# Twelve-head input loads issued as two DMAs of half a row each, in a q·kᵀ kernel

## The chip, the cores and the metric

The kernel runs on one core of a Trainium2 chip. The metric is device time in microseconds (us) of the whole program; less is better. The core has a matrix engine (PE), a vector engine (DVE), a scalar engine (ACT), a general engine (POOL) and a synchronising engine (SP), each with its own stream of instructions; semaphores order them. Data moves between the large memory (DRAM) and the core's on-chip memory (128 partitions) through 16 DMA engines. A DMA is issued by an instruction on an engine's queue: here SP's, which appears in the profile as q1, or ACT's, which appears as q10.

## The reference

For 8 x 12 = 96 heads, each with a q and a k of 1024 rows by 64 columns in float32, the product of all rows with all rows:

```python
def reference(q, k):                      # (8, 12, 1024, 64) each
    return np.einsum('bhid,bhjd->bhij', q, k).astype(np.float32)
```

The inputs are 50.33 MB and the output, 96 matrices of 1024 x 1024 float32, is 402.65 MB.

## The kernel before

The 96 heads are cut into blocks of 2, 2, 4, 8, 8 and then six times 12 heads (`sizes`). For each block, q and k are loaded as float32, cast to float16 by POOL, transposed so that the 64 columns lie on partitions, and multiplied head by head by PE; ACT copies the products from PE's accumulators to an output buffer, and SP issues one store of 4 MB for each head. The kernel writes its own semaphore counts: `Engine.run` makes an instruction wait for a list of events, `Landing` counts the 16 increments that each DMA gives to its semaphore, and `Ring` hands out buffers in turn together with the events that must be over before a buffer is written again.

What matters for the change and for the steps of the prediction:

- **Loads.** `Block.load` (lines 152 to 163) takes an input buffer from the ring `inputs`, which has two (`x_sb`, 24 KB in each partition), waits until its last reader is done, and issues one DMA that puts `R` consecutive rows into each partition (line 160). For twelve heads this is 12 x 1024 / 128 = 96 rows of 64 float32, 24,576 consecutive bytes in each partition. The event that stands for the load is the buffer's semaphore with its count so far. For the first three blocks the data goes into an output buffer that isn't in use yet (lines 330 to 343); those loads, and the two of the first block of eight, are issued by SP at the start. All others are issued by ACT through `next_load` (line 350), q first and then k.
- **When a load is issued.** `LOADS` (line 81) and line 410 put it behind the second group of products of a head: heads 4 and 6 of a block of eight, heads 6 and 8 of a block of twelve. It fetches what the block after the next will use.
- **Casts.** `cast_quads` (line 201) has POOL write float16 into one of two buffers `half`, once the load has landed (line 215) and the transpose that read this buffer before is done. A block of twelve has four chunks, two of q and two of k, each of four casts.
- **Transposes.** `transpose_quads` (line 222) has DVE transpose a chunk (line 230). It also waits for the last matmul of the block two before, since both use the same buffers `qT` and `kT`. They are written into the program during the heads of the block before (line 409).
- **Products.** `scores` (line 239) issues for each head four groups of two row tiles: a weight load (line 309) and two matmuls of 512 columns (line 312) for each tile, then one copy of 128 x 2048 by ACT (line 289). The first group of a block waits for that block's transposes. The copies wait until the output buffer is free, that is until the store of three heads earlier has landed; there are three output buffers. SP waits for the copies and issues the store (line 302).

Of the kernel before, what the change touches and what calls it, by code (L numbers as in the profile page):

```python
# [8 lines left out]
P = 128  # L9
# [50 lines left out]
def kernel(  # L60
# [8 lines left out]
    B, H, S, D = q.shape  # L69
# [4 lines left out]
    flat = [x.rearrange("b h s d -> (b h s) d") for x in (q, k)]  # L74
# [61 lines left out]
    class Block:  # L136
# [15 lines left out]
        def load(self, x, eng, landing=None):  # L152
            events = []
            if self.raw[x] is None:
                buf, events, self.raw_busy[x] = inputs.next()
                self.raw[x] = buf[:, : self.elems]
                landing = input_landing[id(buf)]
            src = flat[x][self.first * S : (self.first + self.N) * S]
            eng.wait(events)
            dma = eng.eng.dma_start(  # L160
                out=self.raw[x], in_=src.rearrange("(p r) d -> p (r d)", p=P)
            )
            self.landed[x].append(landing.start(dma))

        def load_head(self, n, x, eng, landing):
            start = (self.first + n) * S
# [189 lines left out]
    for x in range(2):  # L356
# [7 lines left out]
                out=ident,  # L364
                in_=ident,
# [98 lines left out]
```

## Time and profile before

| | |
|---|---|
| median of 3 runs | 1062.36 us (1062.35 to 1063.84) |
| the profiled execution | 1062.55 us, of which the span from the first to the last instruction is 1060.4 us |
| PE busy | 700.5 us (66% of the span), 1568 instructions |
| ACT busy | 697.0 us (66%) |
| DVE busy | 470.6 us (44%) |
| POOL busy | 345.3 us (33%) |
| DMA traffic | 453.19 MB in 17,583 packets, mean 427 GB/s over the span |
| one copy of 128 x 2048 on ACT (line 289) | 1.86 us, 384 copies (four smaller ones on DVE) |
| store of one head, issue to landing | 21.7 us (median of 96) |
| load of twelve heads, issue to landing | 22.0 us for q, 21.9 us for k (medians of 6 each) |

The page divides the span into 40 slices and gives each engine's busy share in tenths; the row DMA is the mean share of the 16 DMA engines. A packet is what one DMA engine moves in one piece. For the large transfers here, that is one partition's share of a DMA: 32,768 bytes for a store of one head, 24,576 bytes for a load of twelve heads. Each DMA ends with one packet of 4 bytes on each of the 16 engines, the increments of its semaphore. In the list of groups, and in the timeline, a line names the engine, the line of the program, the operation and the buffers, then the number of instructions; in square brackets stands how long the engine was idle ahead of it, and what ended that.

### The profile page before, as it was taken

The page shows a single profiled execution, that of the slowest core. Times are in us where ns is not written, and L with a number is a line of the kernel's source. Part 1 is how long each engine was busy: PE and PEld are TensorE (multiplying, and loading weights), DVE is VectorE, ACT ScalarE, POOL GpSimd, SP SyncE. Part 2 cuts the span into 40 slices and gives each one's busy share as a digit, 9 for nine tenths or more (in the row PEclk, how much of TensorE's full clock was granted, in tenths as well). Part 3 has the DMA queues.
Part 4 walks back from the last instruction along what each step waited for, and adds up shares of the span by engine and source line. Part 5 has one row for each costly group of instructions (what it writes and reads, how often), then busy time and mean ns, then how long its engine had stood idle before and what let it go on. Part 6 is the DMA issues. An engine that isn't in the chain of part 4 may idle for free.

```text
span 1060.4 us, 3258 instructions
## 1 busy us (share of the span) xinstructions
PE 700.5 (66%) x1568; PEld 127.3 (12%) x800; DVE 470.6 (44%) x43; ACT 697.0 (66%) x386; POOL 345.3 (33%) x158
## 2 busy tenths in 40 slices
PE   6876755765577557774577855777557777778770
PEld 2111100110111001110011100111001111111110
DVE  2998602991795006960069600795007950000000
ACT  4766755755678557775577755776557777777771
POOL 7667216436360430704307053160531600000000
DMA  9999999999999999999999999999999999999997
GB/s 376 434 435 434 432 419 430 435 428 431 433 432 428 428 435 430 430 431 423 438 431 429 433 431 434 434 429 422 426 432 435 429 434 434 434 435 430 431 434 336
DMA packets 17583, 453.19 MB, mean 427 GB/s; under 512 B 1952, under 2 KB 1952, under 8 KB 2976
## 3 DMA queue, kind: packets, MB, share of 16 engines
q1 hardware_dynamic: 14976, 410.00, 90.0%
q10 hardware_dynamic: 2592, 42.99, 9.7%
q8 instruction: 9, 0.15, 0.0%
q14 instruction: 6, 0.05, 0.0%
HBM read 50.33 MB, written 402.65 MB: 427 GB/s over the span
## 4 chain that ended last, share of the span: by engine, by line
DMA 71%; ACT 17%; PE 7%; DVE 2%; issue 1%; POOL 0%; ACTq 0%; SPq 0%
DMA out_dram<-o_sb 70%; ACT o_sb L289 17%; PE ps_all L312 7%; DVE kT L230 1%; DVE qT L230 1%; DMA o_sb<-in_q_dram 0%; PE ps_all L244 0%; POOL qT L180 0%; DVE kT L251 0%; ACT kT L251 0%; ACTq L36 0%; SPq L168 0%; SPq L459 0%; SPq L97 0%
## 5 line engine op out<-in xcount | busy, mean ns | idle before, releaser
L289 ACT COPY o_sb<-ps_all 128x2048 f32<-128x2048 f32 (+1 forms) x384 | 694.7, 1859 | 333.0 <-DMA out_dram<-o_sb 301.6
L312 PE MATMUL ps_all<-kT,qT 64*128 64x512 f16 x1536 | 696.4, 617 | 327.8 <-ACT o_sb L289 322.4
L211 POOL CAST half<-x_sb 32x3072 f16<-32x3072 f32 (+1 forms) x128 | 323.4, 2527 | 491.6 <-DMA x_sb<-in_q_dram 242.2
L230 DVE STREAM_TRANSPOSE qT<-half 128x3072 f16<-128x3072 f16 (+1 forms) x16 | 222.9, 14132 | 370.0 <-PE ps_all L312 370.0
L309 PEld LDWEIGHTS <-qT 64*128 64x128 f16 x768 | 124.2, 162 | 896.8 <-issue 889.2
L230 DVE STREAM_TRANSPOSE kT<-half 128x3072 f16<-128x3072 f16 (+1 forms) x16 | 224.2, 14217 | 2.8 <-POOL half L211 2.8
L230 DVE STREAM_TRANSPOSE kT<-kT 128x1024 f16<-128x1024 f16 x2 | 9.3, 4836 | 0.0
L230 DVE STREAM_TRANSPOSE qT<-qT 128x1024 f16<-128x1024 f16 x2 | 9.2, 4784 | 0.0
L211 POOL CAST qT<-o_sb 32x1024 f16<-32x1024 f32 x8 | 8.3, 1034 | 1.2 <-DMA o_sb<-in_q_dram 0.8
L211 POOL CAST kT<-o_sb 32x1024 f16<-32x1024 f32 x8 | 8.3, 1033 | 0.5
L251 DVE COPY qT<-ps_all 128x1024 f16<-128x1024 f16 x2 | 2.5, 1225 | 11.0 <-PE ps_all L244 11.0
L289 DVE COPY o_sb<-ps_all 128x1024 f32<-128x1024 f32 x4 | 4.9, 1225 | 4.4 <-PE ps_all L312 4.4
L244 PE MATMUL ps_all<-ident,qT 128*128 128x128 f16 x16 | 2.1, 310 | 6.7 <-POOL qT L180 6.6
L251 ACT COPY kT<-ps_all 128x1024 f16<-128x1024 f16 x1 | 1.0, 1012 | 4.7 <-PE ps_all L244 4.7
L180 POOL CAST qT<-o_sb 128x512 f16<-128x512 f32 x4 | 2.3, 612 | 3.6 <-DMA o_sb<-in_q_dram 3.6
L251 DVE COPY kT<-ps_all 128x1024 f16<-128x1024 f16 x1 | 1.2, 1225 | 4.4 <-PE ps_all L244 4.4
L251 ACT ACT_TABLE_LOAD x1 | 1.3, 1283 | 2.8 <-issue 2.8
L244 PE MATMUL ps_all<-ident,kT 128*128 128x128 f16 x16 | 2.0, 305 | 0.7 <-ACT o_sb L289 0.7
L180 POOL CAST kT<-o_sb 128x512 f16<-128x512 f32 x4 | 2.3, 613 | 0.4 <-DMA o_sb<-in_q_dram 0.4
L244 PEld LDWEIGHTS ps_all<-ident,qT 128*128 128x128 f16 x16 | 1.5, 140 | 6.9 <-POOL qT L180 6.9
L244 PEld LDWEIGHTS ps_all<-ident,kT 128*128 128x128 f16 x16 | 1.5, 136 | 3.3 <-POOL qT L211 1.6
L359 POOL MEMSET ident<- 128x128 f16 x1 | 0.2, 205 | 0.5 <-SPq L97 0.5
(5 smaller groups left out, 0.7 us busy)
## 6 DMA issues: line engine op xcount, KB each, us to landing
out_dram<-o_sb SPq DMA_DIRECT2D x96, 4096.0 KB, 21.7
x_sb<-in_q_dram ACTq DMA_DIRECT2D x6, 3072.0 KB, 22.0
x_sb<-in_k_dram ACTq DMA_DIRECT2D x6, 3072.0 KB, 21.9
x_sb<-in_q_dram SPq DMA_DIRECT2D x1, 2048.0 KB, 14.6
x_sb<-in_k_dram SPq DMA_DIRECT2D x1, 2048.0 KB, 19.6
x_sb<-in_q_dram ACTq DMA_DIRECT2D x1, 2048.0 KB, 18.3
x_sb<-in_k_dram ACTq DMA_DIRECT2D x1, 2048.0 KB, 19.1
o_sb<-in_k_dram ACTq DMA_DIRECT2D x4, 256.0 KB, 4.7
```

The source lines that it names most:

```text
L180: lambda: nc.gpsimd.tensor_copy(out=rows[:, :, h], in_=self.raw[x][:, h * n : (h + 1) * n].rearrange("p (r d) -> p r d", d=D),),
L211: lambda: nc.gpsimd.tensor_copy(out=dst[q0 : q0 + 32].rearrange("p (r d) -> p r d", d=32), in_=raw[32 * b : 32 * b + 32, c * m : (c + 1) * ...
L230: lambda: nc.vector.transpose(out=dst, in_=buf.rearrange("p (r i) -> p r i", i=32)),
L244: lambda: nc.tensor.transpose(t_ps[:, t], rows[:, t], ident),
L251: lambda: copy(out=dst, in_=t_ps.rearrange("c t m -> c m t")), [done]
L289: lambda: (nc.vector.tensor_copy if by_dve else nc.scalar.copy)(out=dst, in_=ps[:, : w * S]),
L309: return nc.tensor.ldweights(stationary, tile_position=(at, 0))
L312: return nc.tensor.add_instruction(mybir.InstMatmult(name=nc.get_next_instruction_name(), ins=[nc.tensor.lower_ap(moving), nc.tensor.lower ...
L359: cleared = gps.run(lambda: nc.gpsimd.memset(ident, 0.0))
```

## The change

Only `Block.load` is changed. Where a block has more than eight heads, the load is issued as two DMAs in direct succession on the same queue: the first brings the first half of each partition's row of 24,576 bytes, the second the rest. Both count on the same semaphore, and the event that readers wait for is the count after the second. Loads of smaller blocks are issued as before.

```diff
-            src = flat[x][self.first * S : (self.first + self.N) * S]
+            src = flat[x][self.first * S : (self.first + self.N) * S].rearrange(
+                "(p r) d -> p (r d)", p=P
+            )
             eng.wait(events)
-            dma = eng.eng.dma_start(
-                out=self.raw[x], in_=src.rearrange("(p r) d -> p (r d)", p=P)
-            )
-            self.landed[x].append(landing.start(dma))
+            pieces = 2 if self.N > 8 else 1
+            m = self.elems // pieces
+            for i in range(pieces):
+                dma = eng.eng.dma_start(
+                    out=self.raw[x][:, i * m : (i + 1) * m], in_=src[:, i * m : (i + 1) * m]
+                )
+                landed = landing.start(dma)
+            self.landed[x].append(landed)
```

## The prediction, made before the changed kernel ran

> **What bounds the kernel now.** I read the page's slices first, then its table of queues and its chain of waits, then the windows of the stages, then vector engine and loads in the timeline. The slices and queues, from the page:
>
> ```profile
> DMA  9999999999999999999999999999999999999997
> DMA packets 17583, 453.19 MB, mean 427 GB/s; under 512 B 1952, under 2 KB 1952, under 8 KB 2976
> q1 hardware_dynamic: 14976, 410.00, 90.0%
> q10 hardware_dynamic: 2592, 42.99, 9.7%
> DMA 71%; ACT 17%; PE 7%; DVE 2%; issue 1%; POOL 0%; ACTq 0%; SPq 0%
> out_dram<-o_sb SPq DMA_DIRECT2D x96, 4096.0 KB, 21.7
> x_sb<-in_q_dram ACTq DMA_DIRECT2D x6, 3072.0 KB, 22.0
> ```
>
> The 16 DMA engines are busy in every slice, and the two queues' packets fill 90.0 + 9.7 = 99.7% of the span. ACT's 17% and PE's 7% of the chain are no second bound: while ACT refills one output buffer, two stores stand on q1. The packet records say so more sharply: from about 4 us to 1053 us all 16 engines always have a packet in hand. They end one by one from 1053.3 to 1058.6 us, and the last store lands at 1059.1. So the time is the packet time of the engine that ends last, and an edit counts by the DMA engine time that it adds.
>
> The windows lie over the six pairs of loads (131-186 and so on) and the store-only stretches between:
>
> ```profile
> core 0: us, PE busy (x) PEld busy (x) DVE busy (x) ACT busy (x) POOL busy (x), PEclk, DMA share, GB/s
> 96.00:131.00 35.00, 25.74 (x58) 4.70 (x29) 25.18 (x3) 24.41 (x14) 15.10 (x8) 1.00 1.00 432
> 131.00:186.00 55.00, 29.45 (x65) 5.17 (x32) 6.38 (x1) 29.09 (x16) 21.92 (x8) 1.00 1.01 428
> ...
> 388.00:468.00 80.00, 57.78 (x128) 10.34 (x64) 61.29 (x4) 58.15 (x32) 21.92 (x8) 1.00 1.00 433
> 468.00:520.00 52.00, 29.30 (x65) 5.20 (x32) 0.44 (x1) 29.08 (x16) 21.92 (x8) 1.00 1.00 423
> ```
>
> Both kinds are full (share 1.00), yet a stage with loads moves less: weighted by length the six give 427.5 GB/s, the store-only windows 432.6. That is 1.2% of 316 us, or 3.7 us: the only slack in the DMA time that this change can touch.
>
> **The change, part by part.** Twelve loads (six q, six k, of blocks of twelve heads) become 24 DMAs; bytes, order and buffers stay, and the other engines' instructions stand as before.
>
> 1. Packets. A load of twelve heads is 128 packets of 24,576 bytes, eight on each engine. Median packet times in the records are 312 ns for 8,192 bytes, 611 for 16,384, 912 for 24,576 and 1213 for 32,768: 300 ns for every 8 KB, and 12 ns beside them. By that line 12,288 bytes take about 462 ns. The next packet starts 4 ns before the last one's record ends (stores start every 1209 ns), so a packet holds its engine for 458 ns: two are 916, one of 24 KB is 908. Each engine has 12 x 8 = 96 such pieces: 96 x 8 ns = 0.77 us.
>
> 2. Semaphore writes. Each DMA ends with one packet of 4 bytes on each engine. It is recorded with 9 ns, and the next store's data starts 6 ns after it started: 12 more cost about 0.08 us.
>
> 3. The second issue on ACT's queue.
>
> ```profile
> 159.86 1.86 ACT L289 COPY o_sb<-ps_all 128x2048 f32<-128x2048 f32 x1 [5.02 <-DMA out_dram<-o_sb]
> 159.91 0.33 ACTq L160 DMA_DIRECT2D x_sb<-in_k_dram  x1
> 161.62 1.87 ACT L289 COPY o_sb<-ps_all 128x2048 f32<-128x2048 f32 x1
> ```
>
> The issue (0.33 us) runs while the copy before it runs; a second still ends by 160.6, before the next copy at 161.62. Taken: nothing. Without that cover it were 12 x 0.334 = 4.0 us of ACT, which has 2.2 to 5 us idle for a store in each head. SP's queue, which issues the stores, gets no new instruction.
>
> 4. Later landings. In the records q1 and q10 alternate packet by packet on an engine: eight load packets with eight stores between them make 8 x (0.908 + 1.209) = 16.9 us, and the first load's packets run from 136.1 to 152.2. With 16 pieces it is 16 x (0.458 + 1.209) = 26.7 us, so q lands some 10 us later, and k, queued behind it, also about 10. Who waits is POOL's casts, and for them DVE:
>
> ```profile
> 153.79 22.34 POOL L211 CAST half<-x_sb 32x3072 f16<-32x3072 f32 x8 [40.59 <-DMA x_sb<-in_q_dram]
> 179.62 30.95 DVE L230 STREAM_TRANSPOSE qT<-half 128x3072 f16<-128x3072 f16 x2 [55.60 <-PE ps_all L312]
> 210.15 31.14 DVE L230 STREAM_TRANSPOSE kT<-half 128x3072 f16<-128x3072 f16 x2
> 272.06 30.95 DVE L230 STREAM_TRANSPOSE qT<-half 128x3072 f16<-128x3072 f16 x2 [30.77 <-PE ps_all L312]
> ```
>
> POOL's first chunk would be ready at about 175 instead of 165; DVE takes it at 179.6, since it waits for PE. Should DVE start late all the same, this block's transposes end at 241.3 and the block before leaves PE at 272: 30.8 us of cover, some 70 us in later blocks. Beyond it PE would stall for the excess, and the queues stay fed for the two stores already issued. Taken: nothing.
>
> 5. Collisions of loads and stores. In the records the 24 KB packets have a mean of 931 ns against 912; stores in the load stages 1232 against 1214 elsewhere. (1536 x 19 + 1711 x 18) / 16 engines = 3.8 us per engine, which agrees with the windows. No row shows it for 12 KB packets, so I bound it: at best it goes, -3.8 us; at worst it doubles with the packets, +3.8. The long packets stand in the first ten us of a load, more after a store-only stretch (0.25 to 0.76 us of engine time for q) than for the k behind it (0 to 0.16): they go with the start of reading, and the second piece brings no pause and so no new start. I take 0, the row as it is.
>
> Sum: 0.77 + 0.08 = +0.85 us of engine time, all of it on the bound. The profiled execution took 1062.55 us, its span 1060.4, so 2.15 lie around it, which don't change; it stands 0.2 above the median of 1062.36. Forecast: span 1061.2, median 1063.2.
>
> [...]
>
> **The rivals.**
>
> *Collisions go with the number of load packets (slower).* Place: the engines during the loads. Price: up to 3.8 us on top, 1063.2 + 3.8 = 1067.0. For it: each read among stores is a chance to be held up, there are twice as many, and reading lasts 27 us instead of 17. Against it: the second half of a load shows hardly any long packet. It decides from a growth of a third: 0.85 + 1.3 passes 0.2%.
>
> *Thinner reading collides less (faster).* The loads' share of engine time in such a stage falls from 0.908/2.117 = 43% to 0.458/1.667 = 27%. If collisions go with the density of reads, the 3.8 us may nearly go: 1063.2 - 3.8 = 1059.4. It must save over 3 us to pass 0.2%. What it could add is the skew: the 16 landings of a store lie 1.6 us apart before the first loads and 5.5 at the end, partly through the loads; the last engine ends some 3.5 us after the mean. Against it: even with no collision left the gain is 0.3%.
>
> *A fixed cost for each DMA stands open.* If the second DMA waited for the first to land, engines idle: from the last 24 KB packet's end to the landing it is 152.2 to 153.7, 1.5 us; twelve make 18 us, 1081. Against it: q1 has stores queued which would use that time, and the 6 ns above.
>
> *The change doesn't do what it says.* If the two pieces were made into the same 24 KB packets, the time stays at 1062.4. The packet's size now equals the row's run exactly, so I doubt it.
>
> **How the numbers follow.** 0.2% of the time is 2.1 us, about what a measurement of this kernel tells from no change: the bounds are 1060.2 and 1064.5. Chances: forecast 0.46, no change in packets 0.04, together 0.50 within; more collisions 0.28, fixed cost or a wait that I hold to be covered 0.05, together 0.33 slower; fewer collisions and less skew 0.17 faster. The predicted time is the forecast's, 1063.2, with 1061.5 to 1064.5 for this case alone. The range takes both ends of the collisions, 1059.4 to 1067.0, and leaves out the fixed cost.
>
> **What would show it.** q10 with 1536 + 192 = 1728 more packets and the same 42.99 MB; DMA share still 9 in every slice; packets of 12 KB near 462 ns (over 475 the first step is wrong); issue to landing near 32 us instead of 22 for the second pieces; DVE's waits still for PE and not for POOL; no idle of PE for DVE in the blocks of twelve. GB/s in the load windows judges the collisions: about 426 for the forecast, below 422 for more, near 430 for fewer. The prediction is wrong if the DMA row drops below 9 in a slice before the last, or if load windows of equal bytes change their length by over 3 us in sum.

## The result: 0.67% slower, and the profile after

| | before | changed |
|---|---|---|
| median of 6 runs | 1063.01 us | 1069.70 us (1068.22 to 1072.10) |
| ratio to before, 95% interval | | 1.0067 [1.0057, 1.0077] |
| profiled execution, its span | 1062.55, 1060.4 | 1070.06, 1067.9 |

The change costs 6.7 us. The page of the changed kernel, with the rows shown of before (queue rows: packets, MB, share of 16 engines; issue rows: count, KB each, median us to landing):

```profile
DMA  9999999999999999999999999999999999999997
DMA packets 19311, 453.19 MB, mean 424 GB/s; under 512 B 2144, under 2 KB 2144, under 8 KB 3168
q1 hardware_dynamic: 14976, 410.00, 89.9%
q10 hardware_dynamic: 4320, 42.99, 9.5%
DMA 71%; ACT 17%; PE 7%; DVE 2%; issue 1%; POOL 0%; ACTq 0%; SPq 0%
out_dram<-o_sb SPq DMA_DIRECT2D x96, 4096.0 KB, 22.1
x_sb<-in_q_dram ACTq DMA_DIRECT2D x12, 1536.0 KB, 25.4
```

q10 has 1728 packets more for the same bytes, so the loads are split as described. The DMA engines are as full as before, and the chain has the same shares: no new wait in it, the same transfers take longer. q1 didn't change at all in packets or bytes, yet its share of a span that is 7.5 us longer is nearly the same: 90.0% of 1060.4 us are 954 us, 89.9% of 1067.9 are 960. The stores' own packets have become longer, by some 6 us. That is the first reading to take from this pair of pages.

The windows of the changed kernel (same columns as before; the stages with loads are longer now):

```profile
96.00:131.00 35.00, 25.75 (x58) 4.68 (x29) 25.22 (x3) 24.52 (x14) 15.11 (x8) 1.00 1.00 429
131.00:194.00 63.00, 35.20 (x79) 6.16 (x39) 16.14 (x2) 36.38 (x20) 22.41 (x9) 1.00 1.01 427
...
404.00:474.00 70.00, 51.66 (x115) 9.20 (x57) 61.41 (x4) 50.91 (x28) 21.94 (x8) 1.00 1.00 432
474.00:538.00 64.00, 36.77 (x82) 6.50 (x40) 0.28 (x1) 36.39 (x20) 21.94 (x8) 1.00 1.00 420
```

Weighted over all six, the load stages last 380 us (316 before) at 423.6 GB/s (427.5), the store-only ones move 431.8 (432.6). Against the store-only rate the load stages lose 7.2 us where they lost 3.7.

The timeline shows that the later landings found their cover: first POOL and DVE around the first split load, then ACT at the issue of a k load.

```profile
163.89 22.36 POOL L217 CAST half<-x_sb 32x3072 f16<-32x3072 f32 x8 [50.66 <-DMA x_sb<-in_q_dram]
177.85 30.91 DVE L236 STREAM_TRANSPOSE qT<-half 128x3072 f16<-128x3072 f16 x2 [53.85 <-POOL half L217]
208.34 31.14 DVE L236 STREAM_TRANSPOSE kT<-half 128x3072 f16<-128x3072 f16 x2
272.74 30.90 DVE L236 STREAM_TRANSPOSE qT<-half 128x3072 f16<-128x3072 f16 x2 [33.25 <-PE ps_all L318]
```

```profile
157.87 1.87 ACT L295 COPY o_sb<-ps_all 128x2048 f32<-128x2048 f32 x1 [6.28 <-DMA out_dram<-o_sb]
157.92 2.15 ACTq L165 DMA_DIRECT2D x_sb<-in_k_dram  x2
159.63 1.88 ACT L295 COPY o_sb<-ps_all 128x2048 f32<-128x2048 f32 x1
161.68 1.87 ACT L295 COPY o_sb<-ps_all 128x2048 f32<-128x2048 f32 x1 [0.17 <-PE ps_all L318]
```

DVE's first transpose of that block is released by POOL now instead of by PE, but the block's transposes end at 239.5 and the block before leaves PE at 272.7. The two issues take 2.15 us on ACT's queue instead of twice 0.33; the next copies still start in step (159.63), and the third waits 0.17 us for PE, as before.

**Where the 7.5 us of the profiled pair are**, from the records of single packets. What a record lasts beyond the median of its size is called excess here, summed and divided by 16 engines.

```
us per engine                                   before   changed
excess in the load stages: stores of 32 KB        2.07      7.64
                           load packets           1.87      0.21
excess in all records of 8 KB and more            5.3      10.2
mean end of the 16 engines (last store)         1055.5    1060.9
end of the last engine                          1059.1    1066.6
```

A packet of 12,288 bytes takes 460 ns and the next starts 4 ns before its end, so the two cost 912 where one of 24 KB cost 908: 0.4 us for 96 pieces, with the semaphore writes 0.45. The collisions grew by about 4 us in the load stages and moved: they stood half on the load packets, now they stand on the stores. The mean engine ends 5.4 us later, and the last engine stands 5.7 us behind the mean instead of 3.6. Together 7.5.

Within the load stages the excess has a place. The packets of an engine can be told apart by joining each to the one that ends as it starts (where two engines' packets end within a few ns, this can exchange them). One engine of the changed kernel, start in us, length in ns, queue and bytes:

```
748.378  1744  q1  32768     eighth packet of a store
750.118   460  q10 12288
750.574     9  q1  4         that store's semaphore write
750.580   460  q10 12288
751.036  1213  q1  32768     next store
```

In load stages the eighth packets of a store are some 150 to 160 ns over 1213 on the mean, the seventh 30 to 37 and the first two no more than 3. Without load packets beside them eighth packets have next to no excess (under 5 ns on the mean). Around a store's end that lies between two load packets (the eighth packet, the load packets ahead of and behind the semaphore write) the excess is 220 ns on the mean of 185 such ends before and 218 ns of 352 after. The mean price is the same and the number has about doubled, since a load of sixteen packets runs through two stores' ends where eight run through one. That is 2.2 of the 4 us; the rest lies on other store packets beside load packets.

The equal means hide a difference. Before, an end among q's packets cost 382 ns (91 ends) and one among k's only 63 (94 ends). In the changed kernel, in the four pairs of loads whose ends stand clearly apart in time, the four ends of a pair cost 321, 161, 192 and 168 ns in their order. The first is still the dearest, but the later ones are no longer nearly free.

### The profile page after: what moved, and what is told of

Read it like the earlier page. It is cut to its first block, busy times and chain, and to the rows that moved or that the text cites. A ratio compares the mean times of both kernels' runs of the same rounds, so it can differ in the third digit from the quotient of the medians.

```text
span 1067.9 us, 3270 instructions
## 1 busy us (share of the span) xinstructions
PE 700.6 (66%) x1568; PEld 127.2 (12%) x800; DVE 470.4 (44%) x43; ACT 697.5 (65%) x386; POOL 345.6 (32%) x158
## 3 DMA queue, kind: packets, MB, share of 16 engines
q1 hardware_dynamic: 14976, 410.00, 89.9%
## 4 chain that ended last, share of the span: by engine, by line
DMA 71%; ACT 17%; PE 7%; DVE 2%; issue 1%; POOL 0%; ACTq 0%; SPq 0%
DMA out_dram<-o_sb 71%; ACT o_sb L295 17%; PE ps_all L318 7%; DVE kT L236 1%; DVE qT L236 1%; DMA o_sb<-in_q_dram 0%; PE ps_all L250 0%; POOL qT L186 0%; DVE kT L257 0%; ACT kT L257 0%; ACTq L36 0%; SPq L174 0%; SPq L465 0%; SPq L97 0%
## 5 line engine op out<-in xcount | busy, mean ns | idle before, releaser
L257 DVE COPY qT<-ps_all 128x1024 f16<-128x1024 f16 x2 | 2.4, 1224 | 11.1 <-PE ps_all L250 11.1
```

Source lines behind the costliest of these rows:

```text
L257: lambda: copy(out=dst, in_=t_ps.rearrange("c t m -> c m t")), [done]
```

## The experiments

Each kernel was timed beside the kernel before on the same chip. The kernels ran in four groups on different chips, so kernels of different groups are best compared by their ratios. The excerpts are shortened; they are of `Block.load`, or of the line named.

**Packets or DMAs?** First: one DMA again, but of two packets per partition.

```diff
-    x_sb = pool.tile([P, NMAX * S * D // P], F32)
+    x_sb = pool.tile([P, NMAX * S * D // P + 16], F32)
+    if self.N > 8:
+        self.raw[x] = buf.rearrange("p (i e) -> p i e", i=2)[:, :, : self.elems // 2]
+    src = src.rearrange("(p i r) d -> p i (r d)", p=P, i=2)
+    dma = eng.eng.dma_start(out=self.raw[x], in_=src)
```

> Each load of twelve heads is one DMA again, but of two packets of 12,288 bytes per partition (the input buffer has a gap of 32 bytes in the middle and at the end of each row, so that the halves can't be one packet; POOL reads over the gap). Packet theory (what costs is that the load's packets between the stores' are short, so that a store's last packet is held up before its semaphore write; it is the 8th packet of a store that is long in the load stages of the changed kernel, 151 ns more than 1213 on the mean): as slow as the changed kernel, ratio to before 1.0055 to 1.0075, about 1069.5 us, and again some 150 ns on the 8th packets. DMA-count theory (what costs is the second DMA: its issue took 1.2 to 1.9 us on ACT instead of 0.33, and its semaphore writes): as fast as before plus the 0.77 us of packets, ratio about 1.001, 1063.8 us.

1068.87 us, ratio 1.0059 [1.0047, 1.0072]; eighth packets again some 150 ns over. Two lines of its page show that the packets are halved and the DMAs are not:

```profile
q10 hardware_dynamic: 4128, 42.99, 9.5%
x_sb<-in_q_dram ACTq DMA_DIRECT2D x6, 3072.0 KB, 31.3
```

With one DMA for each load nearly all of the cost is there. The second DMA, its semaphore writes and its slow issue are worth at most the 0.8 us that stand between the two kernels, and the intervals overlap.

Second: two DMAs, packets as before.

```diff
-    out=self.raw[x][:, i * m : (i + 1) * m], in_=src[:, i * m : (i + 1) * m]
+    out=self.raw[x][i * P // pieces : (i + 1) * P // pieces],
+    in_=src[i * P // pieces : (i + 1) * P // pieces],
```

> Each load of twelve heads is two DMAs again, but the first brings partitions 0 to 63 and the second 64 to 127, so that the packets are 24,576 bytes, as before the change, and eight per engine. Packet theory: as before, ratio 1.000 to 1.001, about 1063.1 us, and no more than some 50 ns on the 8th packets of stores. DMA-count theory: as slow as the changed kernel, ratio about 1.0065, 1069.7 us.

1093.61 us, ratio 1.0294 [1.0280, 1.0308]: both theories missed by far. The windows of this kernel:

```profile
96.00:131.00 35.00, 25.71 (x58) 4.70 (x29) 26.02 (x3) 24.46 (x14) 15.09 (x8) 1.00 1.00 432
131.00:188.00 57.00, 29.49 (x66) 5.18 (x32) 4.99 (x1) 29.08 (x16) 21.92 (x8) 1.00 1.00 393
```

The load stage falls to 393 GB/s, with the engines full. Its 24 KB packets last 1164 ns in the median, not 912. This experiment changed more than it meant to: each DMA now writes to 64 partitions, where those of the kernel before and of the changed kernel write to all 128. Why the packets are longer was not shown: no other kernel here halves a load by partitions. So this one says nothing on the number of DMAs.

**Does it need two queues?** The loads moved to the stores' own queue, whole and split.

```diff
-    side[1] = side.get(1, []) + [lambda: next_load(act)]
+    side[1] = side.get(1, []) + [lambda: next_load(sp)]
```

> The kernel before, but the loads that ACT issued are issued by SP, so that they stand in the stores' own queue between two stores, and no load packet stands between two packets of one store. Packet theory: the collisions go, 3.8 us of engine time and some of the skew between the engines, ratio 0.994 to 0.997, 1057 to 1060 us. DMA-count theory: no change, 1063 us. If a store behind a load comes too late for its output buffer, slower than before by up to 12 x 7.3 us.

> The changed kernel, with the same move of the loads to SP's queue. Packet theory: short packets cost only what the records show for themselves, so 0.85 us more than the kernel with whole loads on SP's queue, 1058 to 1061 us. DMA-count theory: the second DMA costs as in the changed kernel, some 6.7 us more than the kernel with whole loads on SP's queue.

1064.76 (ratio 1.0021 [1.0012, 1.0030]) and 1064.82 us (1.0022 [1.0013, 1.0031]). Splitting cost nothing that shows (0.06 us) where the load packets stand behind one another between two stores. These lines are from the page of the kernel with split loads on SP:

```profile
q1 hardware_dynamic: 18720, 451.94, 99.1%
q10 hardware_dynamic: 576, 1.05, 0.3%
x_sb<-in_q_dram SPq DMA_DIRECT2D x12, 1536.0 KB, 26.1
```

Nearly all bytes are on q1, twelve q loads of half size among them. So the cost belongs to short load packets *between* a store's packets, not to short packets. The expected gain over the kernel before did not come. The stores' excess falls to 0.7 us in all, but the load packets have 3.6 (whole) and 2.9 us (split); the mean engine ends at 1055.0, close to the 1055.5 of before, and the last at 1061.8.

**How does it go with size?** Four pieces of 6 KB, and pieces of 18 and 6 KB.

```diff
-    pieces = 2 if self.N > 8 else 1
+    pieces = 4 if self.N > 8 else 1
```

> The changed kernel with four pieces of 6,144 bytes per partition instead of two. Own price of the packets: 192 more per engine by 8 ns, and 24 more semaphore writes: 1.7 us over the changed kernel. Store-end theory (the last packet of a store, which is the 8th, is held up when a load packet follows it, and the more the shorter that is: 46 ns on the mean with 24 KB behind it, 171 with 12 KB): by that line some 230 ns with 6 KB, and 48 such ends on each engine instead of 24, so 11 us instead of 4: with the packets about 1078.5 us, ratio 1.014 to 1.018, and most of the excess stands on 8th packets. Rival (any load packet between stores can collide, whatever the place): collisions double again, 7.6 to about 15 us, about 1079 us, spread evenly over a store's eight packets.

```diff
-    m = self.elems // pieces
+    cuts = [0, self.elems * 3 // 4, self.elems] if pieces == 2 else [0, self.elems]
-    out=self.raw[x][:, i * m : (i + 1) * m], in_=src[:, i * m : (i + 1) * m]
+    out=self.raw[x][:, cuts[i] : cuts[i + 1]], in_=src[:, cuts[i] : cuts[i + 1]]
```

> The changed kernel, but the first piece has 18,432 bytes per partition and the second 6,144. Number of packets and of store ends between load packets as in the changed kernel. Store-end theory: 8th packets followed by an 18 KB packet are about 110 ns long over 1213, those followed by a 6 KB packet 230 or more; sum as in the changed kernel, ratio 1.0055 to 1.0075. Rival: no difference by the size that follows.

Four pieces: 1068.97 us, but from 1064.37 to 1072.78 (ratio 1.0058 [1.0035, 1.0081]), where about 1079 was expected by both. Uneven: 1066.53, ratio 1.0033 [1.0020, 1.0046], below what was expected. "The shorter, the more" falls: around a store's end the excess is some 260 to 270 ns with 18 KB packets in the uneven kernel, 2 ns with its 6 KB packets, and 45 ns with 6 KB in the profiled execution of four pieces (which took 1064.76, near its fastest). So in the profiled executions 12, 18 and 24 KB cost 0.2 to 0.3 us for each store's end on the mean and 6 KB next to nothing. That is neither the line that was drawn nor an even spread. No trace shows where the time of the longer runs of four pieces went. With four pieces the cover for later landings runs out as well: k's pieces take 55.6 us to land (median), and PE waits once 5.5 us for a transpose, but the DMA row stays at 9 in every slice but the last.

**Do store ends matter?** Stores of two packets of 16 KB for each partition, as two DMAs or as one, with split loads, with whole loads, and with whole loads on SP's queue.

```diff
-    o_sb = pool.tile([P, NT, S], F32)
+    o_sb = pool.tile([P, 2, NT // 2 * S + 8], F32)
+    dst = of[self.first + n].rearrange("(p i t) j -> p i (t j)", p=P, i=2)
+    for i in range(2):
+        dma = nc.sync.dma_start(out=dst[:, i], in_=buf[:, i, : NT // 2 * S])
```

```diff
+    dst = of[self.first + n].rearrange("(p i t) j -> p i (t j)", p=P, i=2)
+    dma = nc.sync.dma_start(out=dst, in_=buf[:, :, : NT // 2 * S])
```

> The changed kernel, with each store issued as two DMAs of 16,384 bytes per partition (the output buffers have a gap of 32 bytes in the middle and at the end of each row). It has the same packets as the next kernel, but twice as many store ends: 8 packets per engine to each. Both pay 768 more packets by 8 ns, 6.1 us. Store-end theory: 24 ends between load packets on each engine as in the changed kernel, 4.1 us, so about 1076 us, ratio 1.012 to 1.014, and 2 to 3 us slower than the next kernel. Rival: 0.6 us slower than the next one, for the semaphore writes alone.

> The changed kernel, with each store one DMA of two packets of 16,384 bytes per partition (same gap in the buffers), so that a store ends after 16 packets on each engine and not after 8. Store-end theory: 12 ends between load packets on each engine, 2 us instead of 4, about 1073.5 us, ratio 1.009 to 1.011, the excess on 16th packets. Rival: 1075 us or so, 0.6 us under the kernel with two DMAs.

> Loads as before the change (one DMA, 24,576 bytes per partition, on ACT's queue), stores as two DMAs of 16,384 bytes per partition. Theory (the cost goes with the number of store ends that fall between load packets): a load of eight packets per engine passes eight store packets of 16 KB, that is one store end, 12 in all, against 24 with the split loads and 12 with split loads and single stores. The two kernels with split loads stood 9.9 us apart, so here about 5 us between this and the next, this about 1066 to 1070 us. Rival (two DMAs to a store cost by themselves, wherever the loads are): 10 us between this and the next one.

> Loads as before the change, stores as one DMA of two packets of 16,384 bytes per partition: a load passes half a store end, 6 in all. Theory: about 5 us under the kernel with two DMAs to a store, 1062 to 1065 us; split loads on this cost about half of what they cost on the kernel before, 2 to 5 us. Rival: 10 us under the kernel with two DMAs.

> The loads whole and on SP's queue, so that no load packet stands between packets of a store, and stores as two DMAs. Theory: no store end falls between load packets, so only 0.6 us of semaphore writes over the next kernel; both some 4 us over the kernel with whole loads on SP's queue (1064.8), for 768 more packets by 5 ns: about 1069 us. Rival: 10 us over the next kernel, 1076 us or more.

> The loads whole and on SP's queue, stores as one DMA of two packets of 16,384 bytes per partition. Theory and rival: about 1068.5 us; the theories differ in the kernel with two DMAs to a store.

| median us (ratio, interval) | two DMAs to a store | one DMA | apart |
|---|---|---|---|
| split loads, ACT's queue | 1076.47 (1.0132 [1.0119, 1.0145]) | 1066.62 (1.0042 [1.0031, 1.0054]) | 9.9 |
| whole loads, ACT's queue | 1075.88 (1.0105 [1.0087, 1.0124]) | 1064.75 (1.0025 [1.0015, 1.0036]) | 11.1 |
| whole loads, SP's queue | 1070.00 (1.0070 [1.0057, 1.0082]) | 1069.60 (1.0066 [1.0053, 1.0078]) | 0.4 |

With loads between the stores' packets, two DMAs to a store cost 10 to 11 us by the medians and 8.5 to 9.6 by the ratios (the kernel with whole loads on ACT's queue ran from 1070.95 to 1076.27); without, 0.4. So a second DMA to a store, and with it a second end, costs only while loads are mixed in: that part of the theory holds in both directions. Its amounts don't. Split loads with single stores were expected at 1073.5 and took 1066.62. With the number of ends in the loads, whole loads should have shown half the distance of split ones, and they show about as much. By the ratios, splitting the loads costs 2.9 us with two DMAs to a store and 1.8 with one, against 6.7 on the kernel before.

Nor do the records put the distance on the ends: with split loads and two DMAs to a store, an end between load packets has an excess of 88 ns, and the 280 of them make 1.6 us for each engine. The profiled executions are only 5.9 (split) and 8.1 us (whole) apart, since those with one DMA were the longest of their kernels. With split loads the mean engine ends at 1063.7 (two DMAs) and 1062.8 us (one), and the last engine 8.8 and 4.0 us behind it: most of the distance is the lag of the last engine. With whole loads the mean engine ends at 1064.4 and 1059.9 and the last 8.2 and 4.9 us behind it: there all engines pay more than half. What two DMAs to a store cost among loads stays unexplained.

**Each load its share, or the unbroken reading?**

```diff
-    pieces = 2 if self.N > 8 else 1
+    pieces = 2 if self.N > 8 and x == 0 else 1
```

> The changed kernel, but only q's loads are split; k's are single DMAs of 24,576 bytes per partition. Theory (the cost comes from how many store packets, and with them store ends, a load's packets stand between; each split load adds its share): six of twelve loads, so half of 6.7 us: about 1066 us, ratio 1.002 to 1.0045. Rival (the cost comes from q's and k's loads running into each other, one unbroken stretch of 55 us of reading where there were two of 16): that stretch is broken again, so no more than 0.5 us over before.

```diff
-    LOADS = {0: (), 1: (), 2: (1, 3), 3: (4, 6), 4: (4, 6)}
+    LOADS = {0: (), 1: (), 2: (1, 3), 3: (4, 5, 6, 7), 4: (4, 5, 6, 7)}
-    if n in LOADS.get(i, (6, 8)):
+    if n in LOADS.get(i, (6, 7, 8, 9)):
```

Each call of `next_load` issues one piece here.

> The changed kernel, but the second piece of each load is issued one head later than the first (q at heads 6 and 7, k at 8 and 9; in the blocks of eight at 4, 5 and 6, 7), so that the pieces are not directly behind each other and no DMA waits behind another on ACT's queue. Theory: as many load packets stand between store packets as in the changed kernel, so as slow: 1069 to 1071 us, ratio 1.0055 to 1.008. Rival (unbroken reading, or the wait of the second piece behind the first): 1063 to 1065 us.

1066.67 us, ratio 1.0034 [1.0023, 1.0046], and 1070.24 us, ratio 1.0066 [1.0054, 1.0078]. Half the split loads cost half; pieces that are not behind each other cost as much as in the changed kernel. Both as the theory said, and the rival falls. In the first of them, with both sizes in one execution, 172 ends lie between 12 KB packets and 86 between 24 KB ones, with six loads of each: two to one, as counted. But there an end among 24 KB packets cost 352 ns and one among 12 KB packets 193, so both kinds of load paid about 2 us for each engine at their ends: the count alone doesn't set the cost.

## Why the prediction was wrong

The forecast was 1063.2 and the range ended at 1067.0; the kernel takes 1069.7. The prediction's steps in turn:

1. *Packets.* Right, and a little high: 0.4 us instead of 0.77.
2. *Semaphore writes.* 0.08 us, lost in the whole; one DMA of short packets against two (1068.87 and 1069.70 us) shows that nothing large was overlooked.
3. *The second issue on ACT's queue.* Its length was mis-sized: 1.2 to 1.9 us, not 0.33. Its price on the path was right: the copies go on in step.
4. *Later landings.* Right in its price. Second pieces of q land 31.7 us after their issue in the first stage (near 32 forecast), DVE keeps over 30 us of cover, and no product of the later blocks waits for it. One of its signs failed: DVE waits once for POOL, 53.9 us in the first stage, and still starts at 177.85, ahead of the 179.6 of before.
5. *Collisions of loads and stores.* **This is the step that failed.** It read from before that long packets go with the start of reading, and that "the second piece brings no pause and so no new start", and took 0. In the changed kernel the excess does not fade after the start; on the stores it goes on through all 55 us of a q and k pair. Collisions in the load stages grew from 3.9 to 7.9 us for each engine: the upper bound that the step had worked out (+3.8), taken for the worst case. The reading of before was right in that q's loads had most of the excess, but it couldn't tell the start of reading from the end of a store. Before, the one store's end that a load passes stood just ahead of its third, fourth or fifth packet in 157 of 192 cases, and the long load packets were the third to fifth as well. The second piece brought no new start, but it brought a second end, and the later ends of a pair cost 160 to 190 ns each where k's had cost 63. The sign named for this step, the GB/s of the load windows, gave 423.6, between the 426 of the forecast and the 422 for more collisions.

The rival "collisions go with the number of load packets" came true in its size for the mean engine, but its reason was wrong: four pieces have twice the packets again and did not cost more. What doubled was how many store packets, and store ends, a load's packets stand between. Even this rival's price was too low for the time. In the profiled pair the mean engine ends 5.4 us later: 0.45 for the packets, 3.9 for collisions in the load stages and 1.0 for longer packets outside them, where the range's upper end had room for 0.85 and 3.8. On top of that the lag of the last engine grew by 2.1 us; the prediction had a change of the lag in the faster case only, as a smaller one.

The other rivals fall as argued: a fixed cost for each DMA would have shown with split loads on SP's queue (they took 0.06 us more), and the packets did change.

Shown by runs: it is the halved packets and not the second DMA; it needs loads and stores on two queues; each split load adds its share; direct succession plays no part; and a second DMA to each store costs much only among loads. Seen in the records, not separately shown: that some 0.2 us are lost on the mean at each store's end between load packets of 12 to 24 KB. This price isn't constant: it goes from 0.09 to 0.35 us by kernel. Open: what in a DMA engine holds the store's last packet there, why 6 KB packets hardly did it in the one profiled execution while runs with them differ by 8 us, and what decides which engine falls behind; on SP's queue, with only 0.7 us of excess on the stores, the last engine is 6.8 us behind the mean too. None of the fourteen kernels beat the kernel before.

## What to carry to other kernels

Where the DMA engines are full all the time, ask of a split transfer not only what its pieces cost but what it is mixed with and for how long: these two queues alternated packet by packet, and loads of twice the packets had about twice as many ends of the other queue's DMAs between their own packets, 352 where there were 185. A bound that has been worked out for an unknown cost should be weighed, not set to zero because a plausible reading of before says so. Where the engines end apart, as the 16 of the changed kernel did by 10 us (they end their last stores from 1056.5 to 1066.6 us), the time is the last engine's: a change of the mean tells only part.

## What the runs showed of the hardware beyond that

- A second DMA issued right behind another on ACT's queue held the queue's issue for 1.2 to 1.9 us in the changed kernel, where the first took 0.33; in the kernel that issues it a head later it took 0.33 again.
- Halving the loads by partitions instead of by bytes cost far more: 31 us where the changed kernel's halves cost 6.7, with packets of 24 KB as before the change that lasted 1164 ns in the median and not 912.
- The engines did not drift back together in the last store-only stretch, behind all loads: from about 840 us to the end the last engine's lag on the mean goes from 2.4 to 3.6 us before and from 5.4 to 5.7 in the changed kernel. With whole loads on SP's queue it goes from 5.4 to 6.7 there, so not all of the lag arises among loads.
